# A hybrid encoder layer on one core: normalising x after the projections instead of before

## The chip, the cores and the metric

The kernel runs on one core of one Trainium2 chip. The metric is the device time of one execution in microseconds (us), lower is better. Five engines run side by side, each through its own instructions in order, and wait for one another by semaphores: PE (TensorE, matrix products; its weight loads are shown as PEld), DVE (VectorE, elementwise work), ACT (ScalarE, elementwise functions and copies), POOL (GpSimd) and SP (SyncE, which here only issues DMA transfers).

## The reference

One layer over x (1024 tokens, 1024 channels), all in float32. Cut to what matters:

```python
h = x * rsqrt(mean(x*x, axis=-1) + EPS) * norm_g           # RMS norm, one factor per token
proj = h @ w_in                                            # 1024 x 3328 columns
hy_in, g_h, q, k, v, g_a = split(proj)                     # 1536, 512, 512, 128, 128, 512
u = conv_b + sum(pad(hy_in)[:, j:j+L] * conv_w[j] for j in range(3))
hv, hx1, hx2 = split(u, 3)                                 # 512 channels each
z = hx1 * long_conv(hv, k_f[0], bias[0])                   # two-sided filters, by FFT in the reference
z = hx2 * long_conv(z, k_f[1], bias[1])                    # k_f from a three-layer sine MLP over positions
y_a = windowed_sink_attention(rope(rms(q)), rope(rms(k)), v)   # each query sees +-128 tokens
y = concat([rms(z) * silu(g_h), rms(y_a) * silu(g_a)])
out = x + y @ w_out
```

The factor rsqrt(mean(x*x)+EPS) belongs to a token, that is to a row of h, so it can be applied to x or to the rows of proj: `(x * norm_g * r) @ w = r * ((x * norm_g) @ w)`.

## The kernel before

Every float32 product of the projections is made of three matmuls: a value is split into a high part that the fast matmul format holds exactly and the low rest, and hi\*hi, hi\*lo and lo\*hi are added up in PSUM. x is loaded transposed (channels on the 128 partitions) in two halves of 512 tokens, each as 8 chunks of 128 channels. `prepare_x` squares the chunks of a half on ACT (L134, L137), adds the squares on DVE (L138), sums over channels with a matmul by ones (L142), makes the rsqrt on DVE by three Newton steps (`rsqrt`, L71 to L87), spreads it over the partitions by a matmul with the identity (`xr`, L149), and then for each chunk multiplies x by it (DVE L154), rounds to the high part `h` (ACT L158) and subtracts for the low part (L160, in turn on DVE and POOL). Only then can a projection of that half begin.

A projection tile is 128 of the 3328 columns (`half`, L192): 24 matmuls of 512 tokens for each half, into one of two PSUM banks `proj`. Its weights are loaded, split and stored in one of three slots (`weights`, L163). A hyena tile (12 of them, three for each quarter of 128 channels) is copied out of PSUM by ACT (L214), convolved with the three short taps (ACT L218, DVE L220), transposed on PE (`uT`, L230), copied by ACT (L231) and stored to DRAM as `hy`. A gate tile (8) goes through SiLU on ACT (L244, L245). Three q/k/v tiles of 256 columns are copied out by ACT (L290). Beside them the *hyena branch* works: the filter MLP (L332 to L350), and for each quarter two filter spectra (`gen` L403, `dft` L417) and two long convolutions (`fw` L532, much DVE work in the frequency domain, `inv` L571). The third stage is the attention (`smax`, `st`, `pv`) with the output projection (`po`).

The order of the program is written by `weave`: it takes pieces of the hyena branch (a) and of the projection tiles (b) in turn, by a planned cost of each piece, so that b fills PE while a waits for DVE. A scheduling layer then orders each engine's instructions by priority and its own cost model; on the chip each engine keeps that order. What precedes the weave (loading x, the MLP, the first weights, `prepare_x`) is put in order by the string `PLAN`.

## Time and profile before

| | |
|---|---|
| median of 3 runs | 689.33 us (685.95 to 689.79) |
| the profiled execution: its time, its span | 686.11 us, 684.3 us |
| mean granted TensorE clock | 0.985 |
| PE, DVE, ACT, POOL busy | 93%, 77%, 42%, 8% of the span |
| first 40 us: PE, DVE, ACT busy | 14.4, 22.8, 22.0 us |
| 200 to 300 us: PE, DVE, ACT busy | 100.0, 93.9, 35.9 us |

The span is what the trace covers; the time of the same execution is 1.8 us longer. Start times in the trace are counted from the span's start. A matmul's row lasts longer than its share of PE, since matmuls overlap: what one costs in a row of them is the distance from start to start.

### The profile page before, as it was taken

How to read it: one execution, taken by the hardware profiler on the slowest of the kernel's cores; microseconds unless marked ns; L12 is line 12 of the kernel's file. 1: busy time of each engine (PE TensorE's matmuls, PEld its weight loads, DVE VectorE, ACT ScalarE, POOL GpSimd, SP SyncE). 2: the span in 40 equal slices, each digit the busy share in tenths (PEclk: the TensorE clock that was granted, in tenths of full speed). 3: DMA queues.
4: the chain of work that ended last, by engine and by line, in shares of the span. 5: the costliest groups of instructions: out<-in, count | busy, mean ns of one | idle time of the engine just before them, and what ended most of it. 6: DMA issues, size and time to landing. Idle time of an engine off the chain costs nothing.

```text
span 684.3 us, 10610 instructions
## 1 busy us (share of the span) xinstructions
PE 634.8 (93%) x3962; PEld 559.3 (82%) x3962; DVE 525.5 (77%) x1161; ACT 287.8 (42%) x549; POOL 57.0 (8%) x65
## 2 busy tenths in 40 slices
PE   1389899999699999999999999898999899999997
PEld 1356789999589999898999998787888788888886
DVE  3878789698697999979989788353988778966431
ACT  6456343225242323433352434676587534443210
POOL 1242011012010100210100111010000000000000
PEclk9999999999899999999999999999999699999999
DMA  8943634235545314762550745654355732222321
GB/s 288 255 103 82 211 107 108 94 70 117 195 101 154 76 49 139 185 153 78 124 201 1 198 120 151 218 149 129 106 166 161 239 108 79 84 92 95 124 93 61
DMA packets 46888, 90.13 MB, mean 132 GB/s; under 512 B 7154, under 2 KB 15986, under 8 KB 46580
## 3 DMA queue, kind: packets, MB, share of 16 engines
q1 hardware_dynamic: 36656, 73.22, 31.9%
q0 software_dynamic: 7488, 13.63, 11.6%
q10 hardware_dynamic: 2692, 2.60, 1.3%
q8 instruction: 31, 0.51, 0.3%
q14 instruction: 21, 0.17, 0.1%
HBM read 53.78 MB, written 22.02 MB: 111 GB/s over the span
## 4 chain that ended last, share of the span: by engine, by line
PE 74%; DMA 15%; ACT 3%; issue 3%; DVE 3%; POOL 1%; SPq 0%; POOLq 0%; DVEq 0%; ACTq 0%
PE proj L199 8%; PE proj L198 8%; PE proj L200 8%; PE pv L758 5%; PE fw L532 5%; PE dft L417 5%; PE po L845 4%; PE po L846 4%; PE po L847 4%; DMA w_lo<-wraw 4%; PE inv L571 4%; PE qkv L285 3%; PE qkv L286 3%; PE qkv L287 3%; DMA wraw<-in_w_in 2%
## 5 line engine op out<-in xcount | busy, mean ns | idle before, releaser
L199 PE MATMUL proj<-h,w_hi 128*128 128x512 f32 x320 | 128.8, 402 | 1.8 <-DVE h L160 1.0
L198 PE MATMUL proj<-h,w_hi 128*128 128x512 f32 x320 | 127.4, 399 | 2.9 <-ACT h L158 2.9
L200 PE MATMUL proj<-h,w_lo 128*128 128x512 f32 x320 | 126.9, 396 | 0.0
L177 POOL DMA_DIRECT2D w_lo<-wraw x52 | 45.0, 865 | 398.5 <-ACT w_lo L176 343.9
L199 PEld LDWEIGHTS proj<-h,w_hi 128*128 128x128 f32 x320 | 60.7, 190 | 16.3 <-DVE h L160 2.1
L198 PEld LDWEIGHTS proj<-h,w_hi 128*128 128x128 f32 x320 | 60.6, 190 | 15.1 <-ACT h L158 4.0
L200 PEld LDWEIGHTS proj<-h,w_lo 128*128 128x128 f32 x320 | 60.8, 190 | 12.3 <-issue 1.0
L174 ACT CAST w_hi<-wraw 128x512 fp32r<-128x512 f32 x52 | 32.2, 620 | 74.5 <-DMA wraw<-in_w_in 42.4
L286 PE MATMUL qkv<-w_lo,h 128*128 128x256 f32 x192 | 54.6, 284 | 0.0
L285 PE MATMUL qkv<-w_hi,h 128*128 128x256 f32 x192 | 54.6, 284 | 0.0
L287 PE MATMUL qkv<-w_hi,h 128*128 128x256 f32 x192 | 54.4, 283 | 0.0
L758 PEld LDWEIGHTS pv<-vv,pf 128*128 128x128 f32 x352 | 48.2, 201 | 2.3 <-PE bT L720 0.2
L758 PE MATMUL pv<-vv,pf 128*128 128x66 f32 x352 | 47.9, 279 | 0.0
L417 PE MATMUL dft<-eo,d 128*128 128x128 f32 x352 | 46.6, 275 | 0.0
L417 PEld LDWEIGHTS dft<-eo,d 128*128 128x128 f32 x352 | 43.4, 192 | 0.4
L707 DVE CUSTOM_DVE_ANT_0 mj<-smax,mask 128x384 f32<-128x384 f32 (+1 forms) x64 | 33.3, 521 | 13.5 <-PE smax L702 10.4
L176 ACT ACTIVATE w_lo<-wraw 128x512 fp32r<-128x512 f32 x52 | 32.7, 628 | 10.5 <-PE qkv L286 10.5
L532 PE MATMUL fw<-u,d 128*128 128x128 f32 x256 | 33.7, 286 | 3.6 <-DMA u<-hy 3.5
L285 PEld LDWEIGHTS qkv<-w_hi,h 128*128 128x128 f32 x192 | 36.8, 191 | 0.2
L286 PEld LDWEIGHTS qkv<-w_lo,h 128*128 128x128 f32 x192 | 36.8, 192 | 0.1
L287 PEld LDWEIGHTS qkv<-w_hi,h 128*128 128x128 f32 x192 | 36.8, 191 | 0.0
L744 ACT ACTIVATE pf<-st 128x768 f32<-128x768 f32 (+1 forms) x32 | 24.2, 758 | 27.1 <-DVE st L742 24.3
(197 smaller groups left out, 1423.1 us busy)
## 6 DMA issues: line engine op xcount, KB each, us to landing
wraw<-in_w_in SPq DMA_DIRECT2D x52, 256.0 KB, 3.0
w_lo<-wraw POOLq DMA_DIRECT2D x52, 256.0 KB, 3.6
hy<-hraw SPq DMA_DIRECT2D x12, 512.0 KB, 2.6
x<-in_x_t SPq DMA_DIRECT2D x8, 512.0 KB, 5.6
dec<-in_decay SPq DMA_DIRECT2D x8, 512.0 KB, 4.4
g<-hy SPq DMA_DIRECT2D x8, 512.0 KB, 4.3
gt<-graw SPq DMA_DIRECT2D x16, 256.0 KB, 3.4
woraw<-in_w_out SPq DMA_DIRECT2D x16, 256.0 KB, 3.3
```

Of the source, the lines that this page charges most:

```text
L176: nc.scalar.mul(l, raw, -1.0)
L177: nc.gpsimd.dma_start(l.bitcast(F32), raw, accum_op=ALU.add)
L198: nc.tensor.matmul(pt, hi[:, k], xh, start=k == 0, stop=False)
L199: nc.tensor.matmul(pt, hi[:, k], xl, start=False, stop=False)
L200: nc.tensor.matmul(pt, lo[:, k], xh, start=False, stop=k == 7)
L285: nc.tensor.matmul(pt[:, b], hh, hi[:, :, k], start=k == 0, stop=False)
L286: nc.tensor.matmul(pt[:, b], hh, lo[:, :, k], start=False, stop=False)
L287: nc.tensor.matmul(pt[:, b], hl, hi[:, :, k], start=False, stop=k == 7)
L417: nc.tensor.matmul(out, m, eo[:, t, e], start=n == 0, stop=n == len(terms) - 1)
L532: nc.tensor.matmul(pt[:, k, c], self.d[:, t + k, c], u[:, t + k], start=True, stop=True)
L707: V.tensor_tensor_reduce(out=junk[:, 0:nk], in0=pm[:, 0:nk], in1=mask, op0=ALU.add, op1=ALU.max, scale=1.0, scalar=NEG, accum_out=mx[:, 4 ...
L758: nc.tensor.matmul(pv[:, h], probs[:, n, cols], self.vv[:, k0 + n, g], start=n == 0, stop=n == nk - 1)
```

## The change

x is no longer normalised before the projections. `x_high` and `x_low` split x times `norm_g` chunk by chunk as it lands (high part of even chunks on ACT, of odd ones on DVE, all low parts on DVE), and the projections run on that. The sum of squares is still made (`x_square`, in place, two chunks at a time; `x_add`; `x_sum`), and one `rsqrt` for all 1024 tokens gives `rstd` and, spread over the partitions, `row`. Each projection's result is multiplied on its way out of PSUM: hyena and gate tiles on DVE by `row` (`scaled`), where ACT copied or applied SiLU before; q/k/v tiles on ACT by `rstd`, in pieces of 256. The first hyena tiles are written out by hand in `prelude`, half by half of the tokens, with the products of the low weights last for the first two, and `in_order` pins every engine to the written order there. Three banks of the hyena branch and a third staging buffer hold the results until `row` is there. The weave starts at the fourth tile with `AHEAD` units of b counted as done. The transposes of a hyena tile are issued after the first half of the next tile (`put_off`, `late`). The constants come in one transfer, the MLP's bias and frequency are applied by ACT, the first weights are loaded between the chunks of x, and the tables `dft`, `decay`, `dft_neg` after the second half of x.

```diff
-PLAN = "cXYmWwdenabaMMbMMwvv"
...
+AHEAD = 31.2
+
+LATE = 0
...
+    def in_order(self, start):
+        last = {}
+        info = mybir.DependencyInfo(mybir.DependencyClass.NoSync, mybir.DependencyReason.DATA)
+        for i in self.nc.cur_bb.bb.instructions[start:]:
+            if i.engine in last:
+                self.tc.add_manual_dep(i, last[i.engine], info, reason="in_order")
+            last[i.engine] = i.name
...
-        self.gx = cp.tile([P, 8], F32, name="gx")
-        nc.scalar.dma_start(self.gx, a["norm_g"])
...
+        pk = cp.tile([P, 192], F32, name="consts")
+        nc.scalar.dma_start(pk, a["consts"])
...
-    def load_x(self, h, xp):
...
-    def prepare_x(self, h, xp, ps):
...
+    def load_x(self, xp, raw):
+        a, q = self.a, self.nc.sync
+        self.xt = [xp.tile([P, 8, 512], F32, tag="x", name=self.nm("x"), bufs=2) for _ in range(2)]
+        ct = [c for c, _ in self.order[:2]]
+        for h in range(2):
+            for k in range(0, 8, 2):
+                q.dma_start(self.xt[h][:, k : k + 2], a["x_t"][h][:, k : k + 2])
+                if h == 0 and k < 4:
+                    q.dma_start(raw[0][:, 2 * k : 2 * k + 4], a["w_in"][ct[0]][:, 2 * k : 2 * k + 4])
+            if h == 0:
+                q.dma_start(raw[1], a["w_in"][ct[1]])
+    def x_high(self, h, k, e):
+        out, x, g = self.h[h][:, 0, k], self.xt[h][:, k], self.gx[:, k : k + 1]
+        if e == self.nc.vector:
+            e.tensor_scalar(out=out, in0=x, scalar1=g, scalar2=None, op0=ALU.mult)
+        else:
+            e.mul(out, x, g)
+    def x_low(self, h, k):
+        self.nc.vector.scalar_tensor_tensor(
+            out=self.h[h][:, 1, k], in0=self.xt[h][:, k], scalar=self.gx[:, k : k + 1],
+            in1=self.h[h][:, 0, k].bitcast(F32), op0=ALU.mult, op1=ALU.subtract,
+        )
+    def x_square(self, h, k):
+        x = self.xt[h][:, k : k + 2]
+        self.nc.scalar.activation(x, x, AF.Square)
+    def x_add(self, h, k):
+        x = self.xt[h]
+        o, i = (x[:, 0:2], x[:, k : k + 2]) if k else (x[:, 0], x[:, 1])
+        self.nc.vector.tensor_tensor(out=o, in0=o, in1=i, op=ALU.add)
+    def x_sum(self, h, out):
+        for t in range(4):
+            self.nc.tensor.matmul(
+                out[:, 4 * h + t, 0:1], self.xt[h][:, 0, t * P : (t + 1) * P], self.ones[:, 0:1], start=True, stop=True
+            )
+    def x_rows(self, rstd, ps):
+        nc = self.nc
+        for h in range(2):
...
+            nc.scalar.copy(self.row[:, h], row)
+        nc.scalar.copy(self.rstd, rstd)
...
+    def half(self, w, h, evac, lo_last=False, bank=None):
         nc = self.nc
         hi, lo = (x[:, 0] for x in w)
-        pt = self.pj.tile([P, 512], F32, tag="proj", name=self.nm("proj"))
+        pt = (bank or self.pj).tile([P, 512], F32, tag="f" if bank else "proj", name=self.nm("proj"))
         for k in range(8):
             xh, xl = self.h[h][:, 0, k], self.h[h][:, 1, k]
             nc.tensor.matmul(pt, hi[:, k], xh, start=k == 0, stop=False)
             nc.tensor.matmul(pt, hi[:, k], xl, start=False, stop=False)
-            nc.tensor.matmul(pt, lo[:, k], xh, start=False, stop=k == 7)
-            if k < 7 and k % FINE == FINE - 1:
+            if not lo_last:
+                nc.tensor.matmul(pt, lo[:, k], xh, start=False, stop=k == 7)
+            if (k < 7 or lo_last) and k % FINE == FINE - 1:
                 yield 0.65 * FINE
+        for k in range(8 if lo_last else 0):
+            nc.tensor.matmul(pt, lo[:, k], self.h[h][:, 0, k], start=False, stop=k == 7)
+        if h == LATE:
+            self.late()
         evac(h, pt)
         yield 0.65 * min(FINE, 8)
+    def scaled(self, out, pt, h):
+        self.nc.vector.tensor_tensor(out=out, in0=pt, in1=self.row[:, h], op=ALU.mult)
+    def late(self):
+        while self.put_off:
+            self.put_off.pop(0)()
     def hyena_tile(self, n, s, sp, ps):
+        raw = sp.tile([P, S], F32, tag="raw", name=self.nm("hraw"))
+        def evac(h, pt):
+            self.scaled(raw[:, 512 * h : 512 * h + 512], pt, h)
+        yield from self.project(4 * n + s, evac)
+        self.short_conv(n, s, raw, sp, ps)
+    def prelude(self, sp, xp, raw, mlp, w0, ps, tables):
+        nc = self.nc
+        V, A = nc.vector, nc.scalar
+        self.ahead = []
+        del self.order[:2]
+        w = [self.first_slot() for _ in range(2)]
+        for k in range(0, 8, 2):
+            self.x_high(0, k, A)
+            if k < 4:
+                half = slice(2 * k, 2 * k + 4)
+                hi, lo = (x[:, 0, half] for x in w[0])
+                A.copy(hi, raw[0][:, half])
+                nc.gpsimd.tensor_tensor(out=lo, in0=raw[0][:, half], in1=hi.bitcast(F32), op=ALU.subtract)
+            if k == 6:
+                A.copy(w[1][0][:, 0], raw[1])
+            self.x_high(0, k + 1, V)
+            self.x_low(0, k)
+            self.x_low(0, k + 1)
+            if k:
+                self.x_square(0, k - 2)
+        A.mul(w[1][1][:, 0], raw[1], -1.0)
+        nc.gpsimd.dma_start(w[1][1][:, 0].bitcast(F32), raw[1], accum_op=ALU.add)
+        raws = [sp.tile([P, S], F32, tag="raw", name=self.nm("hraw")) for _ in range(3)]
+        banks = {}
+        def part(n, h, last=False):
+            def evac(h, pt):
+                banks[n, h] = pt
+            return self.half(w[n], h, evac, lo_last=last, bank=None if (n, h) in ((0, 0), (1, 0), (2, 1)) else ps)
+        def scaled(n, h):
+            self.scaled(raws[n][:, 512 * h : 512 * h + 512], banks.pop((n, h)), h)
+        def all_of(g):
+            for _ in g:
+                pass
+        all_of(part(0, 0, True))
+        b0 = part(1, 0, True)
+        for _ in range(4):
+            next(b0)
+        self.x_high(1, 0, A)
+        self.x_square(0, 6)
+        for k in range(0, 8, 2):
+            if k:
+                self.x_high(1, k, A)
+            self.x_high(1, k + 1, V)
+            self.x_low(1, k)
+            self.x_low(1, k + 1)
+        all_of(part(0, 1))
+        for k in range(0, 8, 2):
+            self.x_square(1, k)
+        next(mlp)
+        for k in (2, 4, 6, 0):
+            self.x_add(0, k)
+        next(mlp)
+        w.append(self.weights(*self.order.pop(0)))
+        tables()
+        ss = ps.tile([P, 8, 2], F32, tag="g", name=self.nm("xss"))
+        self.x_sum(0, ss)
+        all_of(b0)
+        next(mlp)
+        for k in (2, 4, 6, 0):
+            self.x_add(1, k)
+        b1 = part(1, 1)
+        next(b1), next(b1)
+        self.x_sum(1, ss)
+        next(mlp)
+        r = self.rsqrt(xp, ss[:, :, 0:1].rearrange("p a b -> p (a b)"), 8, 1.0 / DM)
+        next(mlp)
+        all_of(b1)
+        self.x_rows(r, ps)
+        next(mlp)
+        self.ahead.append(self.weights(*self.order.pop(0)))
+        for n in range(2):
+            for h in range(2):
+                scaled(n, h)
+        all_of(part(2, 0))
+        self.short_conv(0, 0, raws[0], sp, ps)
+        for _ in mlp:
+            pass
+        for _ in w0:
+            pass
+        scaled(2, 0)
+        all_of(part(2, 1))
+        scaled(2, 1)
+        self.late()
+        self.short_conv(1, 0, raws[1], sp, ps)
+        self.short_conv(2, 0, raws[2], sp, ps)
+    def short_conv(self, n, s, raw, sp, ps):
...
+        def transposes():
+            for h in range(2):
+                pt = ps.tile([P, 4, P], F32, tag="g", name=self.nm("uT"))
+                for k in range(4):
+                    t = 4 * h + k
+                    nc.tensor.transpose(pt[:, k, :], taps[:, t], self.ident)
+                nc.scalar.copy(u[:, 4 * h : 4 * h + 4, :], pt)
+            nc.sync.dma_start(self.hy[n, s], u)
+            self.stored += 1
+        self.put_off.append(transposes)
...
-                    nc.scalar.activation(raw, pt, AF.Silu)
+                    self.scaled(raw, pt, h)
+                    nc.scalar.activation(raw, raw, AF.Silu)
...
+        if half == LATE:
+            self.late()
...
-            nc.scalar.copy(raw[:, 512 * n : 512 * n + 512], pt.rearrange("p a b c -> p (a b c)"))
+            for b in range(2):
+                j = 4 * half + 2 * n + b
+                cols = slice(512 * n + 256 * b, 512 * n + 256 * b + 256)
+                nc.scalar.mul(raw[:, cols], pt[:, b].rearrange("p b c -> p (b c)"), self.rstd[:, j : j + 1])
...
-            V.tensor_scalar(
-                out=y, in0=pt, scalar1=fb[:, l : l + 1], scalar2=fb[:, 3:4], op0=ALU.add, op1=ALU.mult
-            )
+            nc.scalar.activation(y, pt, AF.Identity, bias=bf[:, l : l + 1], scale=fb[:, 3:4])
+            yield
...
-            sp = Defaults(pool(left, "stage", 1), raw=2, sc=1)
+            sp = Defaults(pool(left, "stage", 1), raw=3, sc=1)
...
-                ta = tb = 0.0
+                ta, tb = 0.0, done
...
+                    w0, w1 = (self.filter_weights(o, fw, keep, ps) for o in range(2))
+                    start = len(nc.cur_bb.bb.instructions)
+                    self.constants(cp)
+                    raw = [xp.tile([P, 8, P], F32, tag="xw", name=self.nm("xw"), bufs=2) for _ in range(2)]
+                    self.load_x(xp, raw)
+                    next(mlp)
+                    next(w0)
+                    def tables():
+                        nc.sync.dma_start(self.d, a["dft"])
+                        nc.sync.dma_start(self.dec0, a["decay"][0])
+                        nc.sync.dma_start(self.dn, a["dft_neg"])
+                    self.prelude(sp, xp, raw, mlp, w0, ps, tables)
+                    self.in_order(start)
+                    run_all(w1)
...
-            rest = weave(hyena_branch(), chain(*(tile_of(*t) for t in order[: len(order) - LASTG + 1])), SHARE, LEAD)
+            tiles = [tile_of(*t) for t in order[3 : len(order) - LASTG + 1]]
+            rest = weave(hyena_branch(), chain(*tiles), SHARE, LEAD, AHEAD)
```

The order that the built programs have on the engines shows this at three places. First PE's start. Before (`xss` is the sum of squares, `xr` the spread factor, `proj_484` the first half of tile 0, `h_89` and `h_90` the two halves of h):

```order
L142 MATMUL xss_208<-ones,xa_185 128x1 x4
L149 MATMUL xr_229<-ident,rsy_216 128x128
L142 MATMUL xss_257<-ones,xa_234 128x1 x2
...
L198 MATMUL proj_484<-h_89,w_hi 128x512
L199 MATMUL proj_484<-h_89,w_hi 128x512
L200 MATMUL proj_484<-h_89,w_lo 128x512
...
L149 MATMUL xr_278<-ident,rsy_265 128x128 x4
L332 MATMUL mlp_307<-mlp_in 128x512
```

With the change (`proj_190` and `proj_249` are the two halves of tile 0, `proj_215` the first half of tile 1; pairs and triples stand eight times each):

```order
L221 MATMUL proj_190<-h_89,w_hi 128x512
L222 MATMUL proj_190<-h_89,w_hi 128x512
...
L228 MATMUL proj_190<-h_89,w_lo 128x512 x8
L221 MATMUL proj_215<-h_89,w_hi 128x512
...
L221 MATMUL proj_249<-h_90,w_hi 128x512
L222 MATMUL proj_249<-h_90,w_hi 128x512
L224 MATMUL proj_249<-h_90,w_lo 128x512
...
L479 MATMUL mlp_280<-mlp_in 128x512
L164 MATMUL xss_307<-ones,x_141 128x1 x4
L228 MATMUL proj_215<-h_89,w_lo 128x512 x8
L481 MATMUL mlp_322<-mh_320,mlp_in 128x512
```

PE's first instructions were the sums of squares; now they are projections, and `xss` stands behind 65 matmuls. Second, DVE inside a long convolution. Before (end of the forward butterfly, the two products with the filter's spectrum, and the short taps of a hyena tile between them):

```order
L520 SCALAR_TENSOR_TENSOR X_604<-gm_616,ml_606 128x2x128 x2
L220 SCALAR_TENSOR_TENSOR hsc_690<-hraw_689,conv_w,hsc_690 128x1023
L553 TENSOR_TENSOR Y_623<-X_604,kt_429 128x2048
L220 SCALAR_TENSOR_TENSOR hsc_690<-hraw_689,conv_w,hsc_690 128x1023
L554 TENSOR_TENSOR X_604<-X_604,kt_429 128x2048
```

With the change, at the same place of a later convolution:

```order
L666 SCALAR_TENSOR_TENSOR X_901<-gm_913,ml_903 128x2x128 x2
L354 SCALAR_TENSOR_TENSOR hsc_1480<-hraw_1417,consts,hsc_1480 128x1023
L699 TENSOR_TENSOR Y_920<-X_901,kt_817 128x2048
L354 SCALAR_TENSOR_TENSOR hsc_1480<-hraw_1417,consts,hsc_1480 128x1023
L700 TENSOR_TENSOR X_901<-X_901,kt_817 128x2048
L235 TENSOR_TENSOR hraw_1484<-proj_1495,row 128x512
L702 TENSOR_TENSOR X_901<-X_901,Y_920 128x8x128
L703 TENSOR_TENSOR X_901<-X_901,Y_920 128x8x128
L235 TENSOR_TENSOR hraw_1484<-proj_1677,row 128x512
```

The evacuations of the projections (`hraw<-proj,row`), which stood on ACT, stand between the steps of the convolution. Third, PE where the transposes of the fifth hyena tile are. Before they stood ahead of the `fw` matmuls of the third convolution:

```order
L199 MATMUL proj_1577<-h_89,w_hi 128x512
L200 MATMUL proj_1577<-h_89,w_lo 128x512
L198 MATMUL proj_1577<-h_89,w_hi 128x512
...
L230 MATMUL uT_1552<-ident,hsc_1486 128x128 x4
L230 MATMUL uT_1558<-ident,hsc_1486 128x128 x3
L532 MATMUL fw_1249<-u_1244,d 128x128 x4
```

With the change they stand inside the second half of the sixth tile:

```order
L221 MATMUL proj_1677<-h_90,w_hi 128x512
L222 MATMUL proj_1677<-h_90,w_hi 128x512
L366 MATMUL uT_1520<-consts,hsc_1480 128x128 x4
L366 MATMUL uT_1526<-consts,hsc_1480 128x128 x4
L224 MATMUL proj_1677<-h_90,w_lo 128x512
```

The transposes moved about one and a half half-tiles of projection work behind the short taps that they read.

115 lines of the change are left out of this document (27 added, 88 removed).

## The prediction

> **What bounds the kernel now.** I read the page first, then the windows by stage, the waits and the timeline of the start.
>
> ```profile
> PE 634.8 (93%) x3962; PEld 559.3 (82%) x3962; DVE 525.5 (77%) x1161; ACT 287.8 (42%) x549; POOL 57.0 (8%) x65
> 0.00:85.30 85.30, 54.02 (x239) 40.41 (x240) 60.93 (x110) 43.98 (x74) 20.89 (x23) 1.00 0.66 189
> 128.00:180.00 52.00, 46.49 (x337) 43.41 (x335) 43.72 (x84) 16.84 (x40) 5.16 (x6) 0.97 0.47 127
> 180.00:224.00 44.00, 43.77 (x267) 39.46 (x267) 37.07 (x60) 13.95 (x24) 3.44 (x4) 0.96 0.40 110
> 224.00:266.00 42.00, 42.00 (x328) 40.56 (x329) 40.83 (x77) 14.21 (x34) 1.72 (x2) 1.00 0.32 101
> 266.00:308.50 42.50, 42.50 (x276) 38.46 (x275) 38.35 (x63) 15.89 (x27) 6.88 (x8) 1.00 0.58 143
> 308.50:352.70 44.20, 43.53 (x285) 39.34 (x285) 41.55 (x65) 18.31 (x41) 3.44 (x4) 1.00 0.48 142
> 352.70:397.50 44.80, 44.79 (x343) 43.03 (x344) 39.33 (x75) 14.38 (x23) 4.30 (x5) 1.00 0.40 108
> 428.00:684.30 256.30, 244.55 (x1441) 209.13 (x1439) 160.64 (x529) 122.15 (x241) 3.44 (x4) 0.97 0.40 127
> ```
>
> The columns after the window's length are PE, PEld, DVE, ACT and POOL busy. From 180 to 397.5 us, one long convolution with its filter in each window, PE has no gap to speak of; DVE is 84 to 97% busy. In the attention, from 428 us, PE is 95% busy and DVE 63%. So PE sets the pace with DVE close behind, and what PE loses at the start is lost for good. There it waits:
>
> ```profile
> PE xss L142 <- DVE xa L138: 14.0, 1, 14.0
> PE xr L149 <- DVE rsy L87: 10.1, 2, 6.2
> PE proj L198 <- ACT h L158: 2.9, 3, 1.6
> 39.35 0.63 PE L198 MATMUL proj<-h,w_hi 128*128 128x512 f32 x1
> 39.77 0.58 PE L199 MATMUL proj<-h,w_hi 128*128 128x512 f32 x1
> 40.42 0.39 PE L198 MATMUL proj<-h,w_hi 128*128 128x512 f32 x1
> 40.65 0.40 PE L199 MATMUL proj<-h,w_hi 128*128 128x512 f32 x1
> ```
>
> 24 us go by for the sum of squares and its rsqrt, and until 40 us a projection matmul costs 0.42 us from start to start, afterwards 0.23.
>
> **The start, step by step.** x arrives as before, so I take its pace from when ACT could use the last chunk of half 0 and the first of half 1:
>
> ```profile
> 5.78 0.63 ACT L134 ACTIVATE xa<-x 128x512 f32<-128x512 f32 x1 [3.08 <-DMA gx<-in_norm_g]
> 9.90 0.63 ACT L137 ACTIVATE xsq<-x 128x512 f32<-128x512 f32 x1 [0.70 <-DMA x<-in_x_t]
> 13.99 0.63 ACT L134 ACTIVATE xa<-x 128x512 f32<-128x512 f32 x1 [0.81 <-DMA x<-in_x_t]
> 19.57 1.15 ACT L137 ACTIVATE xsq<-x 128x512 f32<-128x512 f32 x2 [1.29 <-DMA x<-in_x_t]
> L154 DVE SCALAR_TENSOR_TENSOR x<-x,gx,xr 128x512 f32<-128x512 f32 x16 | 11.6, 736 | 0.0
> L346 DVE TENSOR_SCALAR my<-my 128x512 f32<-128x512 f32 x3 | 1.3, 422 | 0.1
> L556 DVE TENSOR_TENSOR X<-X,Y 128x1024 f32<-128x1024 f32 x8 | 9.8, 1222 | 0.1
> L138 DVE TENSOR_TENSOR xa<-xa,xsq 128x512 f32<-128x512 f32 x14 | 9.7, 691 | 6.4 <-ACT xsq L137 5.7
> L344 DVE SCALAR_TENSOR_TENSOR my<-mk,my 128x512 f32<-128x512 f32 x3 | 2.0, 681 | 0.0
> L84 DVE TENSOR_TENSOR rst<-rsy 128x8 f32<-128x8 f32 x6 | 1.0, 164 | 0.1
> tab<-in_rope ACTq DMA_DIRECT2D x1, 256.0 KB, 5.4
> ```
>
> The first half MB was there by 5.8 us, 2 MB by 9.9, 3 MB by 14.0, 4.5 MB by 19.6. With the change 0.5 MB of weights and the 0.3 MB of a rope table with its factors, whose issue ACT's queue now does first of all, come with half 0, so it is there at 12.5 us and half 1 at 21. DVE needs for two chunks one high part (0.42, as L346) and two low parts (0.74, as L154), 1.9 us: half 0 is split at 14.4, half 1 (four times 1.9, from 16.7, when ACT's first high part is there) at 24. PE's last 24 matmuls on half 0 (8 low-weight ones of tile 0, 16 of tile 1) take some 7 us, half of the time at the slow pace: 21.5. The 24 on half 1 end with the splitting, at 25.
>
> Then DVE leads: `x_add` three times 1.22 and once 0.69, 4.35 us for each half; the MLP's five operations 2.6 us for each layer (two as L344, three as L346); the rsqrt twelve small ones of 0.16, 2 us. In the pinned order 24 + 4.35 + 2.6 + 4.35 + 2.6 + 2 = 40. PE behind it runs the MLP's layers, `xss`, the second tile's rest, and the third MLP layer waits for ACT's sine until 38.6; then 0.95, 12 matmuls 2.7 and the eight `xr` some 1.8: 44. The tables, behind x on SP's queue, are issued about 24 us and come well before the dft. From there PE has its operands: 48 matmuls of tile 2 at 0.227 and one `e0p` (0.95) end at 56. Tile 2 ended at 96.3 before, but PE had by then done more of the hyena branch, so I compare at one point of equal work: the first `fw` and dft done, the first half of tile 3 and 8 matmuls more. That is 103.5 us before:
>
> ```profile
> 85.30 1.13 PE L532 MATMUL fw<-u,d 128*128 128x128 f32 x8 [2.59 <-DMA u<-hy]
> 103.54 0.39 PE L200 MATMUL proj<-h,w_lo 128*128 128x512 f32 x1
> 65.72 0.95 PE e0p L379 x2
> 73.85 7.03 DMA hy<-hraw
> 122.28 4.02 PE dft L417 x36
> 109.53 0.28 PE L285 MATMUL qkv<-w_hi,h 128*128 128x256 f32 x1
> 110.25 0.28 PE L285 MATMUL qkv<-w_hi,h 128*128 128x256 f32 x1
> ```
>
> With the change from 56: `e0p` 0.95, 24 + 8 projection matmuls 7.3; 44 instructions of dft, 32 of `fw`, 16 transposes and 16 of `gen` at the 0.112 of the dft row, 12.1; and some 2 us of waiting for `u`, which goes through DRAM as before (between nothing and the 7 us that its store took last time): 78.3. **PE gains 25.2 us.** The short half 0 first, the pinned order and the moved tables are in this sum; the single constants transfer and the MLP's scaling on ACT (three operations like L245 below, 0.72 each) hide in it behind DVE, uncovered 2 us.
>
> **What the change adds later.** From tile 3 on every evacuation of a hyena or gate tile costs DVE an operation:
>
> ```profile
> L405 DVE TENSOR_TENSOR eo<-gen,dec 128x512 f32<-128x512 f32 x32 | 20.9, 681 | 0.8 <-PE gen L404 0.5
> L214 ACT COPY hraw<-proj 128x512 f32<-128x512 f32 x24 | 14.0, 583 | 20.3 <-PE proj L200 15.7 <-DMA hy<-hraw 4.5
> L245 ACT ACTIVATE graw<-graw,gn 128x512 f32<-128x512 f32 x16 | 11.5, 721 | 0.2
> 113.90 0.89 PE inv L571 x8
> 422.69 1.06 PE inv L571 x8
> ```
>
> An operation out of PSUM like it is L405, 0.68 us, of ACT's copy 0.58. The Trainium skill speaks against the move ("VectorE: DVE Perf Modes", Specifications: VectorE sits closer to SBUF, ScalarE closer to PSUM), and the two rows agree: the 18 evacuations counted next would cost 10.5 us by ACT's row and cost 12 by DVE's, on an engine with less room. By the built order 18 stand between the first and the last `inv`: 18 x 0.68 = 12 us, 1.7 for each of seven convolutions. DVE had 240.9 us in the six windows from 128 to 397.5, 40.1 each; now 41.8. PE's share: first `inv` at 78.3 + 16 projection matmuls and 181 of q/k/v (0.12 each: six between the two rows above) = 103.6, against 113.9, and its last at 422.7 - 25.2 = 397.5 if it never waits: 42.0 each. DVE would be 99.6% busy. The fullest window before is 97% (40.83 of 42.0), so I take 41.8 / 0.97 = 43.1, which costs 7 x 1.1 = **7.6 us** of the gain. The bounds: nothing, if DVE fits, and 33 us, if it is no fuller than its mean before (240.9 / 269.5 = 89%, 46.8 each). The 12 q/k/v evacuations stay on ACT, each now two pieces of 256 by a factor (by L245 some 0.4 each) for one copy like L214, and hide, with ACT some 35% busy; uncovered, 12 x 0.2, 2 us.
>
> The late transposes remove one wait and move a store:
>
> ```profile
> PE uT L230 <- DVE hsc L220: 5.5, 1, 5.5
> ```
>
> It is in the 128 to 180 window, the longest. The next convolution there needed its input through SP's queue at 174 to 180 us anyway, so I credit nothing; bounds 0 and 5.5. In the attention stage 14 evacuations more on DVE (9.5 us) lie in its 37% of idle time.
>
> **Sum:** span 684.3 - 25.2 + 7.6 = 666.7, with the 1.8 us around it 668.5. The profiled execution (686.11) lies near the lowest of the runs, 3.2 us under their median, and so may this.
>
> **Rivals.**
> *PE keeps all of it.* DVE's idle before was waiting for PE (from 180 us on PE has no gap), so it may fill up freely; with the transposes' wait gone too, 686.1 - 25.2 - 0 to 5.5 = 655 to 661. Against it: 99.6%.
> *The branch falls behind.* The projections are ahead by 15 us of work, and where they have run ahead PE lacks filler: an average of 44.2 us for a convolution costs 15 us: 676. For it: a butterfly is a chain of DVE operations that nothing shortens.
> *The clock stays slow.* PE, paced by DVE chunk by chunk, is never busy long enough and keeps 0.42 us from start to start: the 24 matmuls from 14.4 end at 24.5, the next 24 at 35 instead of 25, and what hangs on them (MLP, `xr`) follows some 8 us later: 676. For it: from 27 to 40 us the rows stood at 0.63 with gaps between them; against it, the 24 in a row. The Trainium skill ("TensorE: Matmul & The Clock Gate", Part 1) says that PE starts at half clock until a window of some 3.4 us has been busy; the two distances above agree, and by that rule alone the stream from 14.4 would be released by about 21, not later.
> *Slower.* In-order DVE waits at each evacuation for its projection, with the convolution's chain behind it, and PE then waits at `inv`. The place is the second order shown. DVE stays at 89%: 668.5 - 7.6 + 33 = 694. It decides from 45.6 us for a convolution ((422.7 - 103.6) / 7, DVE 92% full). For it: ACT stood 15.7 us waiting for those same results.
> *No change that can be told*: the same at 45 us, 683 to 690.
>
> **Numbers.** The forecast (661 to 674) 0.48, all kept 0.17, branch behind or slow clock 0.18, no change 0.07, slower 0.10. A measurement of this kernel tells about 0.5%, 3.4 us, from no change: faster 0.83, same 0.07, slower 0.10. The range 655 to 684 holds the first three and leaves the two last.
>
> **What would show it.** First projection matmul near 7 us, `xr` over by 44, tile 2 by 56, the first `fw` near 70, the first `inv` near 104, then 43 us for each; DVE over 95% busy from 104 to 405 with `hraw<-proj,row` rows of 0.68; PE's first 0.23 us distance before 20 us. Wrong if the last `inv` is after 415 (DVE's waits), if half 0 is split after 17 (the transfers), or if PE has long waits on `u` or `w_lo`.

## The result, and the profile after

The changed kernel takes **708.6 us** (708.25 to 709.55) against 689.6 for the kernel before on the same chip: a ratio of 1.028, 95% interval 1.024 to 1.033. It is slower, and the forecast of 668.5 was wrong in sign. The profiled execution took 708.25 us, its span is 706.4.

The busy times of the engines on the page of the changed kernel:

```profile
PE 643.1 (91%) x3962; PEld 561.5 (79%) x3962; DVE 542.5 (77%) x1180; ACT 278.7 (39%) x525; POOL 50.2 (7%) x57
```

Three windows of it (the start to the first inverse transform, from there to the end of the last one, the rest), with the columns as before: length, PE, PEld, DVE, ACT, POOL busy, granted clock, DMA share and GB/s.

```profile
0.00:111.90 111.90, 97.58 (x552) 80.80 (x552) 86.71 (x137) 52.98 (x82) 17.47 (x19) 0.98 0.60 176
111.90:445.00 333.10, 304.11 (x1989) 275.55 (x1990) 288.75 (x506) 100.33 (x201) 29.30 (x34) 0.97 0.43 114
445.00:706.40 261.40, 241.37 (x1423) 205.12 (x1421) 167.07 (x539) 125.39 (x243) 3.47 (x4) 0.96 0.39 122
```

The same three stages of the kernel before:

```profile
0.00:113.70 113.70, 82.36 (x409) 65.59 (x410) 86.42 (x147) 56.24 (x94) 24.32 (x27) 1.00 0.61 171
113.70:428.30 314.60, 308.18 (x2118) 284.86 (x2117) 278.66 (x487) 109.40 (x214) 29.23 (x34) 0.99 0.44 121
428.30:684.30 256.00, 244.25 (x1438) 208.84 (x1437) 160.43 (x529) 122.15 (x241) 3.44 (x4) 0.97 0.40 127
```

Read the counts first. At the first inverse PE has 552 matmuls behind it where it had 409: the head start is there. At the end of the last inverse it has 2541 behind it against 2527, 16.7 us later: the head start has been used up on nothing. PE's idle time per stage is the length less the busy time: 14.3, 29.0 and 20.0 us, where it was 31.3, 6.4 and 11.8. So 17.0 us were gained at the start, and 22.6 and 8.3 lost behind it. Another 8.3 us is PE's own work: the same number of instructions is busy for 643.1 us instead of 634.8, at a lower granted clock (0.969 against 0.985).

The six longest waits of PE between the first inverse and the last, changed kernel (us in total, times, longest):

```profile
PE fw L678 <- DMA u<-hy: 9.6, 3, 6.3
PE proj L221 <- DVE hraw L235: 5.1, 3, 3.0
PE qkv L426 <- DVE hraw L235: 3.1, 2, 1.6
PE uT L366 <- DVE hsc L354: 2.8, 1, 2.8
PE dft L563 <- ACT fc L588: 2.8, 2, 2.1
PE fw L678 <- ACT fc L588: 2.7, 1, 2.7
```

and these were all of them before:

```profile
PE uT L230 <- DVE hsc L220: 5.5, 1, 5.5
PE fw L532 <- DMA u<-hy: 0.9, 2, 0.7
```

The second and third rows are of a new kind: a *projection* waits for the multiplication that empties an earlier projection's bank of PSUM. (`proj` and `qkv` take turns in two banks.) The longest of these waits, in the timelines of PE and then of DVE:

```profile
330.22 0.39 PE L222 MATMUL proj<-h,w_hi 128*128 128x512 f32 x1
330.45 0.39 PE L224 MATMUL proj<-h,w_lo 128*128 128x512 f32 x1
333.86 0.50 PE L221 MATMUL proj<-h,w_hi 128*128 128x512 f32 x1 [3.02 <-DVE hraw L235]
334.20 0.52 PE L222 MATMUL proj<-h,w_hi 128*128 128x512 f32 x1
334.51 0.63 PE L224 MATMUL proj<-h,w_lo 128*128 128x512 f32 x1
...
337.07 0.63 PE L224 MATMUL proj<-h,w_lo 128*128 128x512 f32 x1
337.50 0.50 PE L221 MATMUL proj<-h,w_hi 128*128 128x512 f32 x1
337.84 0.39 PE L222 MATMUL proj<-h,w_hi 128*128 128x512 f32 x1
```

```profile
329.16 0.69 DVE L642 TENSOR_TENSOR ml<-df 128x512 f32<-128x512 f32 x1
329.76 0.42 DVE L652 TENSOR_TENSOR X<-ef 128x256 f32<-128x256 f32 x1
...
332.44 0.76 DVE L666 SCALAR_TENSOR_TENSOR X<-gm,ml 128x256 f32<-128x256 f32 x2
333.11 0.69 DVE L235 TENSOR_TENSOR hraw<-proj,row 128x512 f32<-128x512 f32 x1
333.71 2.29 DVE L699 TENSOR_TENSOR Y<-X,kt 128x2048 f32<-128x2048 f32 x1
...
342.77 0.69 DVE L235 TENSOR_TENSOR hraw<-proj,row 128x512 f32<-128x512 f32 x1
```

One bank was complete at 325.4 us, the other at 330.8. DVE is in the middle of a butterfly, empties the first at 333.1 and the second, behind the products with the spectrum, at 342.8. PE stands still for 3.0 us; then its matmuls go up to 0.43 us from start to start until 337.8 instead of 0.23: the ten from 333.86 take 4.0 us instead of 2.3, and the granted clock from 334 to 338 us is 0.57. The Trainium skill describes such a pair ("TensorE: Matmul & The Clock Gate", section "A second HAM failure mode: psum-queue depth-cycling": PE that cycles through PSUM banks and idles briefly between groups of matmuls loses its clock again and again). At this place the trace agrees, with 3.0 us of standing and 1.7 of slow matmuls. Not every wait is followed by slow ones: after 2.7 us of waiting for `u` at 127.0 us the `fw` matmuls stand at 0.11 us from start to start, after 6.3 us at 274.8 at 0.21.

Counted in the same timelines (24 matmuls to a half tile), the last 18 hyena halves lie complete in their bank for 7.5 us on average, from the end of the last matmul until they have been taken out; before, with ACT's copies, for 1.6.

### The profile page after: what moved, and what is told of

Its sections match the earlier page's. It is cut to its first block, busy times and chain, and to the rows that moved or that the text cites. A ratio compares the mean times of both kernels' runs of the same rounds, so it can differ in the third digit from the quotient of the medians.

```text
span 706.4 us, 10583 instructions
## 1 busy us (share of the span) xinstructions
PE 643.1 (91%) x3962; PEld 561.5 (79%) x3962; DVE 542.5 (77%) x1180; ACT 278.7 (39%) x525; POOL 50.2 (7%) x57
## 4 chain that ended last, share of the span: by engine, by line
PE 49%; DVE 18%; DMA 13%; ACT 4%; issue 3%; ACTq 0%; SPq 0%; DVEq 0%
PE pv L904 5%; PE po L991 4%; PE po L993 4%; PE po L992 4%; DMA w_lo<-wraw 4%; PE proj L221 4%; PE proj L222 3%; PE proj L224 3%; PE fw L678 3%; DMA u<-hy 3%; PE qkv L426 2%; PE qkv L427 2%; PE qkv L428 2%; DMA wraw<-in_w_in 2%; PE dft L563 2%
## 5 line engine op out<-in xcount | busy, mean ns | idle before, releaser
L221 PE MATMUL proj<-h,w_hi 128*128 128x512 f32 x320 | 132.8, 415 | 12.6 <-ACT w_hi L266 7.5
L222 PE MATMUL proj<-h,w_hi 128*128 128x512 f32 x320 | 130.9, 409 | 0.8 <-DVE h L147 0.8
L224 PE MATMUL proj<-h,w_lo 128*128 128x512 f32 x304 | 122.5, 403 | 0.0
L221 PEld LDWEIGHTS proj<-h,w_hi 128*128 128x128 f32 x320 | 62.9, 197 | 27.0 <-ACT w_hi L266 7.5
L222 PEld LDWEIGHTS proj<-h,w_hi 128*128 128x128 f32 x320 | 62.5, 195 | 15.8 <-DVE h L147 4.0
L200 POOL DMA_DIRECT2D w_lo<-wraw x48 | 41.4, 862 | 411.5 <-ACT w_lo L199 392.1
L224 PEld LDWEIGHTS proj<-h,w_lo 128*128 128x128 f32 x304 | 58.4, 192 | 10.9
L197 ACT CAST w_hi<-wraw 128x512 fp32r<-128x512 f32 x48 | 29.7, 618 | 92.3 <-PE proj L222 58.9
L678 PE MATMUL fw<-u,d 128*128 128x128 f32 x256 | 36.4, 301 | 14.0 <-DMA u<-hy 11.0
L904 PEld LDWEIGHTS pv<-vv,pf 128*128 128x128 f32 x352 | 45.3, 192 | 3.5 <-PE st L883 0.9
L678 PEld LDWEIGHTS fw<-u,d 128*128 128x128 f32 x256 | 34.1, 213 | 16.4 <-issue 11.2
L904 PE MATMUL pv<-vv,pf 128*128 128x66 f32 x352 | 44.6, 271 | 0.7 <-DVE rsy L97 0.5
L890 ACT ACTIVATE pf<-st 128x768 f32<-128x768 f32 (+1 forms) x32 | 24.2, 758 | 32.1 <-DVE st L888 29.8
```

The source lines that it names most:

```text
L197: nc.scalar.copy(h, raw)
L200: nc.gpsimd.dma_start(l.bitcast(F32), raw, accum_op=ALU.add)
L221: nc.tensor.matmul(pt, hi[:, k], xh, start=k == 0, stop=False)
L222: nc.tensor.matmul(pt, hi[:, k], xl, start=False, stop=False)
L224: nc.tensor.matmul(pt, lo[:, k], xh, start=False, stop=k == 7)
L678: nc.tensor.matmul(pt[:, k, c], self.d[:, t + k, c], u[:, t + k], start=True, stop=True)
```

## The experiments

All times are medians, all ratios go against the kernel before, which took 688.9 to 689.8 us beside them.

**First: DVE's operations, or the order?** The first theory was that DVE works without a gap between a forward and an inverse transform, so that each eviction lengthens this chain by its 0.69 us. Its rivals: the put-off transposes and a blocked SP queue make `u` late (the 9.6 us above); or any new order of the filler moves the stalls about.

```diff
 # hyena_tile / gate_tiles of the change
-            self.scaled(raw[:, 512 * h : 512 * h + 512], pt, h)
+            self.nc.scalar.copy(raw[:, 512 * h : 512 * h + 512], pt)
...
-                    self.scaled(raw, pt, h)
-                    nc.scalar.activation(raw, raw, AF.Silu)
+                    nc.scalar.activation(raw, pt, AF.Silu)
```

> The change, with the hyena (from the fourth tile) and gate results evicted by ACT again: a plain copy, and SiLU straight from PSUM. The multiplication by 1/rms of these tiles is left out, so DVE has 34 operations of 0.69 us less and ACT 20 copies of 0.58 more. Chain theory (the time goes where DVE works without a gap between a forward and an inverse transform, and each eviction on DVE lengthens it): 18 x 0.69 = 12.4 us between the first and the last inverse come back, and up to 5 in the attention: 691 to 697. Order theory (put-off transposes and a blocked SP queue make u late, the evictions hide): not under 703. Luck theory (every new order of the filler moves the stalls about): anything, with stalls at other places than before and no relation to the 12.4.

**682.6 us**, ratio 0.990 (0.987 to 0.993): 26 us come back, more than the chain theory could explain with 12.4 and up to 5. (The multiplication of these tiles is left out here.)

```diff
 # short_conv of the change
-        self.put_off.append(transposes)
+        transposes()
```

> The change, with a hyena tile's transposes made at once, as in the kernel before, not half a tile later. Chain theory: the same as the change, 705 to 712. Order theory: the u transfers come earlier, the 6.3 us stall at 275 us goes and some of the 4 to 5 us lost at the early convolutions: 695 to 701. Luck theory: a move of several us either way, with stalls at other places.

**702.7 us**, ratio 1.021 (1.015 to 1.026). 6 us come back, although the first `fw` now starts at 90.1 us instead of 75.5: the transposes of the first three tiles now stand in the pinned order of the start. No theory had that.

```diff
 # hyena_tile / gate_tiles of the kernel before
-            nc.scalar.copy(raw[:, 512 * h : 512 * h + 512], pt)
+            nc.vector.tensor_tensor(out=raw[:, 512 * h : 512 * h + 512], in0=pt,
+                in1=view(self.ones, 0, [[0, 4], [1, P]]), op=ALU.mult)
...
-                    nc.scalar.activation(raw, pt, AF.Silu)
+                    nc.vector.tensor_tensor(out=raw, in0=pt, in1=view(self.ones, 0, [[0, 4], [1, P]]), op=ALU.mult)
+                    nc.scalar.activation(raw, raw, AF.Silu)
```

> The kernel before, with its hyena and gate results evicted by DVE (a multiplication by ones, same result) in place of ACT's copy and SiLU. Chain theory: 24 + 16 operations of some 0.69 us, 20 or so of them between the first forward transform and the last inverse: 700 to 709 against 689.6. Order theory: not over 694, DVE has gaps enough. Luck theory: either way, not near 689.6 + 14.

**718.0 us**, ratio 1.042 (1.037 to 1.047): 28 us more. That one edit of the change alone costs more than the whole change, and more than the chain theory's 20. The rest of the change is worth some 7 to 9 us of gain (718.0 to 708.6; 689.6 to 682.6).

Both edits of the change together (the multiplication left out again):

> The change with both: ACT evicts (multiplication by 1/rms of the later tiles left out) and the transposes made at once. What is left of the change is the early start, the shorter split and the pieces of the q/k/v evictions. Chain theory: as with ACT's evictions alone, 690 to 697. Order theory: 690 to 697 too, but then the transposes have moved it and not the evictions. If the head start of PE (25 us) were worth its time: 668 to 675. Luck theory: not the sum of the two single moves.

**692.5 us**, ratio 1.005 (1.002 to 1.008). The two single moves do not add up (-26 and -6 give 676.7): here the same step of the transposes costs 10 us. Each edit also draws a new order of the filler, and part of what it does may be that.

**Second: DVE's time, or the bank?** The chain theory now asked for 0.76 us per operation. The new one: DVE's time is not the matter, but *when* in-order DVE comes to empty the bank. To part them, ACT empties the bank and the multiplication, of the same length, is done afterwards in SBUF, on DVE as here or on POOL (`gpsimd` in the last line):

```diff
 # hyena_tile of the change, and the same for the gates ahead of their SiLU
-            self.scaled(raw[:, 512 * h : 512 * h + 512], pt, h)
+            r = raw[:, 512 * h : 512 * h + 512]
+            self.nc.scalar.copy(r, pt)
+            self.nc.vector.tensor_tensor(out=r, in0=r, in1=self.row[:, h], op=ALU.mult)
```

> The change, with every later hyena and gate result copied out of PSUM by ACT and multiplied in SBUF by DVE; the result is the reference's. DVE's work stays (34 operations of some 0.69 us), but a projection's bank is free as soon as ACT has copied it. If the loss is DVE's time as such: 704 to 712, no better than the change. If it is the bank that is kept until the in-order DVE comes to it (PE waits 8 us for evictions at the projections from 112 us to the last inverse, twice that with the clock's loss): 684 to 692.

**682.5 us**, ratio 0.988 (0.985 to 0.992). The busy times of this kernel's page:

```profile
PE 641.1 (94%) x3962; PEld 563.7 (83%) x3962; DVE 541.2 (79%) x1180; ACT 288.2 (42%) x553; POOL 46.9 (7%) x57
```

Its three stages as windows:

```profile
0.00:114.50 114.50, 98.67 (x556) 82.09 (x556) 86.62 (x137) 54.47 (x85) 14.11 (x19) 0.97 0.58 172
114.50:440.00 325.50, 316.12 (x2072) 288.29 (x2073) 291.84 (x510) 122.54 (x242) 32.74 (x38) 0.98 0.46 125
440.00:681.00 241.00, 226.26 (x1337) 193.27 (x1335) 162.70 (x535) 111.16 (x228) 0.00 (x0) 0.94 0.36 122
```

DVE's multiplication in its groups by line (busy us, mean ns of one, idle before):

```profile
L249 DVE TENSOR_TENSOR hraw<-hraw,row 128x512 f32<-128x512 f32 x18 | 12.3, 689 | 0.0
```

All waits of PE between its inverses:

```profile
PE fw L682 <- DMA u<-hy: 6.1, 2, 3.3
PE dft L567 <- ACT fc L592: 2.4, 1, 2.4
PE fw L682 <- DVE uv L596: 0.8, 1, 0.8
```

DVE is busy as long as in the change (541 and 542 us) with operations of the same 0.69 us, ACT has more to do, and 26 us are gone: exactly where nobody multiplied (682.6). So **in this kernel DVE's 34 operations cost nothing as time.** (One pair of kernels shows this; in the kernel before, further down, the same step leaves 11.6 us.) The waits for `hraw` are gone, and a half tile lies 1.0 us in its bank. 83 matmuls more are done beside the convolutions (2072 against 1989) and 86 fewer are left behind them. The stretch between the inverses is 7.6 us shorter all the same, and the one behind them 20.4 us: PE is busy there 15.1 us less (226.26 against 241.37) and idle 5.3 us less. The chain theory has fallen.

> The change, with every later hyena and gate result copied out of PSUM by ACT and multiplied by the row of 1/rms in SBUF by POOL; the result is the reference's. If the loss is DVE's 34 operations, and POOL's work does not slow DVE: 682.6 as where ACT evicted and nobody multiplied, plus 0 to 4 for the longer way to a tile's transposes: 683 to 687. If POOL's 34 operations slow DVE's beside them (1.51 us against 0.42 in one place of the kernel before): 690 to 700.

**712.0 us**, ratio 1.031 (1.028 to 1.034): worse than the change. DVE runs 1146 instructions, as many as where nobody multiplied, but is busy for 545.3 us instead of 523.2; the last section shows two of the operations that grew. How the 29 us divide between this and POOL's own length was not tried.

Only the hyena tiles' results emptied by ACT, without the multiplication, the gates by DVE as in the change:

> The change, with only the hyena tiles' results (from the fourth tile; 18 operations, all before the last inverse) copied by ACT without the multiplication; the gates' 16 stay on DVE, nearly all in the attention stage. If each DVE eviction costs the same wherever it stands (26 us for 34): 18 x 0.76 = 14 come back, 693 to 697. If only those in the convolutions' chain count: 682 to 687. If only those in the attention: 703 to 709.

**694.1 us**, ratio 1.006 (1.004 to 1.009): 14.5 us come back for the 18 hyena evictions, and by difference the other 11.5 for the gates' 16. The expectation has nearly all of these in the attention, but in this trace 8 of them start before the last inverse ends, at 444.2 us, and PE waits 3.4 us for two of these. The prediction had booked the gates at nothing.

```diff
 # short_conv: only the hand-written first three tiles keep their transposes put off
         self.put_off.append(transposes)
+        if at_once:
+            self.late()
```

> The change, with the transposes of the fourth and later hyena tiles made at once; in the first three, by hand, they stay where the change put them. Where all were made at once the first forward transform came at 90.2 us instead of 75.5 and the time fell by 6 us all the same, so here the start is kept (75 to 77) and the rest is gained: if the put-off transposes cost time in the steady part, 690 to 700; if they do not (the 6 us came from the filler's new order), 704 to 712.

**700.5 us**, ratio 1.015 (1.010 to 1.019): 8 us come back when the steady part of this kernel makes its transposes at once. The first `fw` stays at 75.6 us. Whether the transposes' place does it or the new order was not parted.

**Third: keep the bank, take the time away.** To the kernel with ACT's copies and DVE's multiplications in SBUF comes a read of one column of the bank on DVE:

```diff
             self.nc.scalar.copy(r, pt)
+            self.nc.vector.tensor_copy(self.tiny, pt[:, 0:1])
```

> The kernel in which ACT copies a result out of PSUM and DVE multiplies it in SBUF (682.5 us), and beside ACT's copy DVE reads one column of the same bank into a scratch element that nobody uses: 34 operations of 128x1, some 0.06 to 0.16 us each, 2 to 6 us in all. The result is unchanged. If the loss comes from the bank that is kept until in-order DVE comes to it, the tiny read keeps it as long as the change does: 700 to 709. If it comes from anything else (DVE's time, the way of the rows, a lucky order): 682 to 689.

**696.2 us**, ratio 1.011 (1.004 to 1.017), between the two ranges: 13.7 us of the 26 come with an operation that takes 0.15 us. Its group, two of PE's waits between the inverses, and the windows of the last two stages:

```profile
L250 DVE COPY tiny<-proj 128x1 f32<-128x1 f32 x18 | 2.7, 148 | 2.4 <-ACT hraw L249 2.4
```

```profile
PE proj L222 <- DVE tiny L250: 3.8, 3, 2.7
PE qkv L433 <- DVE tiny L250: 2.2, 2, 1.1
```

```profile
111.90:435.60 323.70, 299.91 (x1987) 270.49 (x1986) 290.06 (x530) 111.93 (x223) 29.34 (x34) 0.98 0.43 117
435.60:693.20 257.60, 243.61 (x1423) 207.21 (x1422) 166.74 (x549) 129.83 (x253) 3.48 (x4) 0.96 0.38 124
```

Its trace is the change's in three things: PE waits for the bank again, 1987 matmuls lie beside the convolutions (1989), 1423 behind them (1423). What it does not bring lies mostly in the convolutions (323.7 against 333.1 us), where the two kernels' orders differ.

The same step in the kernel before: ACT copies its hyena and gate results, and DVE multiplies them by ones in SBUF.

> The kernel before, in which ACT copies the hyena and gate results out of PSUM and DVE then multiplies them in SBUF by ones (same result). DVE has the same 40 operations more as where it evicted by itself (718 us). If the kept bank is the cause there too: 687 to 695, close to the kernel before. If DVE's time is: 712 to 720.

**700.5 us**, ratio 1.018 (1.011 to 1.024), outside both ranges: 17.5 of the 28 us come back, 11.6 stay. In that kernel ACT now waits 12.2 us for the multiplication ahead of `hsc`, and it has two staging tiles `raw` where the change has three. Between the inverses PE also waits twice for ACT at a bank, 2.4 and 2.1 us, which it never did there in the kernel before. That these make up the rest was not tried.

> The kernel in which ACT copies and DVE multiplies in SBUF (682.5 us), with the transposes of the fourth and later hyena tiles at once. With DVE's evictions this step alone brought 8 us. If it acts by itself (u is stored sooner): 672 to 678. If it only mended what the kept banks spoiled: 680 to 686. If every new order of the filler is a draw: as well 690.

**683.2 us**, ratio 0.990 (0.988 to 0.993): with ACT's copies the step that brought 8 us brings nothing.

```diff
-AHEAD = 31.2
+AHEAD = 15.0
```

> The change, with the number by which the weave counts the first three tiles as done at 15 instead of 31.2, so that projections come earlier against the hyena branch; nothing else. If the loss is the kept bank: 703 to 714, since every later eviction still waits for DVE. If the change was only an unlucky draw among the orders: under 698 or over 718.

**699.7 us**, ratio 1.016 (1.010 to 1.021). 9 us, between the two expectations; one number of the weave can do that much.

**Fourth: a third bank.** If the kept bank is what costs, one bank more should do what ACT's copies did, with every eviction left on DVE.

```diff
-NG, NF = 3, 3
+NG, NF = 2, 3
...
+    def bank(self, shape, name):
+        self.turn += 1
+        if self.turn % 3 == 2 and self.third is not None:
+            return self.third.tile(shape, F32, tag="p", name=self.nm(name))
+        return self.pj.tile(shape, F32, tag="proj", name=self.nm(name))
```

> The change with its evictions on DVE, and a third bank of PSUM for the projections until the attention begins; it is taken from the three banks that the transposes and the like share (NG 3 to 2). If the loss comes from a bank that is kept until in-order DVE comes to it, a third bank lets PE go on meanwhile: 684 to 697. If not: 702 or more, since the others have a bank less.

**682.6 us**, ratio 0.991 (0.988 to 0.994), with every eviction still on DVE. The window between its inverses, and PE's waits for a bank in it:

```profile
115.20:436.10 320.90, 309.99 (x2040) 283.39 (x2039) 290.29 (x509) 104.87 (x208) 31.10 (x36) 0.98 0.46 123
```

```profile
PE proj L221 <- DVE hraw L241: 0.7, 1, 0.7
PE qkv L432 <- DVE hraw L241: 0.4, 1, 0.4
```

A half tile still lies 9.1 us in its bank until DVE comes, but PE waits 1.1 us for it instead of 8.2, and 51 matmuls more fit beside the convolutions.

> The same third bank where ACT copies out of PSUM and DVE multiplies in SBUF (682.5 us). ACT frees a bank in time, so by the theory of the kept bank nothing is gained: 680 to 687.

**689.0 us**, ratio 1.000 (0.997 to 1.003): no gain where ACT empties the banks in time, rather 6 us lost.

> ACT copies, DVE multiplies in SBUF (682.5 us), and the weave's 31.2 is 15. With DVE's evictions this step brought 9 us. If it acts by itself (projections earlier beside the convolutions): 672 to 678. If with DVE's evictions it only drew another order: 679 to 689.

**694.7 us**, ratio 1.005 (1.001 to 1.009): 12 us *slower*, outside what was expected; the number that brought 9 us to one kernel takes 12 from the other.

The change with `NG` at 2 and nothing else:

> The change with two shared banks for transposes and the like in place of three, and no third bank for the projections: the other half of the third-bank kernel by itself. By the theory of the kept bank this alone gains nothing: 704 to 715. If it comes below 698, the third bank's result is the draw of a new order.

**709.9 us**, ratio 1.029 (1.024 to 1.033). So 27.3 us lie between two kernels that differ by the third bank alone, with the order that comes of it.

The pairs together, in us:

| otherwise like | DVE empties the bank | ACT does, DVE multiplies in SBUF | difference |
|---|---|---|---|
| the change | 708.6 | 682.5 | -26.1 |
| the change, later transposes at once | 700.5 | 683.2 | -17.3 |
| the change, 15 for 31.2 | 699.7 | 694.7 | -5.0 |
| the kernel before, with multiplications | 718.0 | 700.5 | -17.5 |
| the change, third bank | 682.6 | 689.0 | +6.4 |

In the four pairs with two banks the sign is the same. The size is not: edits that leave the evictions where they are moved the time by up to 12 us either way, and the smallest of the four differences, 5.0 us, lies within that. What remains open is how the 26 us divide between PE's waits on the chip, with the clock behind them, and the order in which PE's instructions were put at build time, which in the change and with the tiny read leaves more matmuls behind the last inverse (1423 in both, against 1337 where ACT empties the banks and DVE reads none of them). In the pair made from the kernel before, that shift is small (1449 against 1431) and the difference is still 17.5 us. The runs show both effects and do not part them.

The kernel with ACT's copy and DVE's multiplication in SBUF computes the reference's result and is faster than both: 682.5 us, 1.2% under the kernel before.

## Why the prediction was wrong, point by point

**The start: right in kind, 8 us too early.** The matmuls of half 0 begin at 7.53 us (forecast 7). Half 0 is split at 15.6 (14.4) and half 1 at 24.2 (24), though the low part takes 0.87 us where the row of another operation gave 0.74. Behind that the lateness grows: the last `xr` is out at 47.4 (44), the first `fw` comes at 75.5 (70), the first `inv` at 111.9 (103.6). The first 3.4 us of it can be read: ACT's sine is there at 40.1 instead of 38.6, and the MLP layer and the twelve matmuls between it and `xr` take 5.3 us instead of 3.65. The rest was not taken apart.

```profile
L147 DVE SCALAR_TENSOR_TENSOR h<-x,consts,h 128x512 fp32r<-128x512 f32 x16 | 13.3, 873 | 1.9 <-ACT h L144 1.9
40.12 1.48 PE L481 MATMUL mlp<-mh,mlp_in 128*128 128x512 f32 x2 [2.32 <-ACT mh L497]
41.83 0.63 PE L222 MATMUL proj<-h,w_hi 128*128 128x512 f32 x1
42.26 0.63 PE L224 MATMUL proj<-h,w_lo 128*128 128x512 f32 x1
75.52 1.13 PE L678 MATMUL fw<-u,d 128*128 128x128 f32 x8 [1.37 <-DMA u<-hy]
```

The "PE gains 25.2 us" was 17.0 by PE's idle time up to the first inverse; 8.3 us of lateness there is the same difference.

**The slow clock: rightly held unlikely where it was put, overlooked where it came.** The 0.23 us distance is there from 18.5 us, and the 24 matmuls on half 1 end at 27.6 us, not at 35 as this rival had it. But once PE had waited 2.3 us for ACT's sine, its matmuls stood at 0.43 us from start to start until 44 us (the middle rows above), with a granted clock of 0.60 from 40 to 44.3 us. This is where about half of the 3.4 us came from by which `xr` was late.

**"What PE loses at the start is lost for good": this step failed.** It took PE's 100% for the pace. Before, PE's only waits between the inverses were 6.4 us, none of them for a bank. A head start of filler is worth its time only while the filler can go on, and the change made PE wait for banks. And even where ACT frees the banks in time, little of the head start is left. In the profile of the 682.5 us kernel PE is idle 15.5 us less at the start than before, but 6.0 us more behind it, and its own work takes 6.3 us more (641.1 against 634.8) at a granted clock of 0.967 against 0.985. So the span is only 3.3 us shorter, and the medians 7.1. Why the granted clock is lower there stays open.

**The 7.6 us for the evictions: the wrong quantity.** The step charged 18 x 0.68 us to DVE's capacity, and asked whether DVE could be 97% full. (In the trace 16 evictions of hyena tiles and 6 of gates start between the first inverse and the end of the last.) As evictions the 34 operations cost 26 us; in SBUF, behind ACT's copies, they cost nothing in this kernel (682.5 against 682.6). What counted was not their length but their place in DVE's order: a bank was held 7.5 us instead of 1.6. The convolutions took (439.6 - 111.9) / 7 = 46.8 us each against 43.1, just the upper bound of 33 us, but with DVE at 288.75 / 333.1 = 87% and PE as the one that waits. The bound assumed a DVE no fuller than before, and so it came out (87% against 89%), but because PE stood waiting for banks and for `u`, not because DVE waited at the evictions: that it was met is luck. Nor do the prediction's two rows for the evictions show that DVE's operation is the longer one because it reads PSUM: with both inputs in SBUF it takes 0.689 us, with one in PSUM 0.687.

**The row that spoke and was read the wrong way.** "ACT stood 15.7 us waiting for those same results" was put down as a sign that DVE would wait too. It said that ACT was free when a result was ready, so that the bank was empty 1.6 us later on average. DVE, 87% busy, had it empty 7.5 us later. In the change DVE waited 0.2 us for those results between the first inverse and the last; they waited for DVE.

**The slower rival** had the sign and, at 694, part of the size, and gave the mechanism in reverse: DVE does not wait at an eviction for PE, PE waits at the next projection for DVE. It also stopped at the convolutions. The gates' evictions, which the prediction let lie in DVE's "37% of idle time" in the attention, were worth 11.5 us; 10 of the 16 start behind the last inverse.

**The late transposes** were credited with nothing, bounded by a gain of 5.5. With the later ones made at once, and with the order that this drew, 8 us came back in this kernel and nothing where ACT empties the banks; no bound to the other side had been given.

**The q/k/v pieces** were right: 0.47 us each, and no wait of PE on them in the steady part.

## What to carry to other kernels

When an instruction that frees a shared buffer moves to another engine, do not only price its length against that engine's idle share: ask what stands ahead of it in that engine's order, and how long the buffer then stays full against the time in which the rotation comes round. A copy by an engine that waits anyway, with the arithmetic done later, can be worth more than the operation it adds; so can one more buffer. And where the order is made by a planner, take two or three neighbouring orders of each version before believing a difference of one or two per cent.

## What the runs showed of the hardware that was not expected

POOL was no help. Its multiplication of 128x512 in SBUF took 2.7 us on average where DVE needs 0.69, and DVE's own operations grew beside it. The kernel with POOL's multiplications:

```profile
L249 POOL TENSOR_TENSOR hraw<-hraw,row 128x512 f32<-128x512 f32 x18 | 48.1, 2674 | 94.2 <-ACT hraw L248 87.9 <-issue 6.3
L356 DVE SCALAR_TENSOR_TENSOR hsc<-hraw,consts,hsc 128x1023 f32<-128x1023 f32 x24 | 35.6, 1483 | 6.8 <-ACT hsc L354 6.7
L555 DVE TENSOR_TENSOR eo<-gen,dec 128x512 f32<-128x512 f32 x32 | 20.9, 682 | 0.7 <-PE gen L554 0.7
L703 DVE TENSOR_TENSOR Y<-X,kt 128x2048 f32<-128x2048 f32 x8 | 20.4, 2546 | 0.1
```

and the change:

```profile
L354 DVE SCALAR_TENSOR_TENSOR hsc<-hraw,consts,hsc 128x1023 f32<-128x1023 f32 x24 | 30.8, 1283 | 2.4 <-ACT hsc L352 2.3
L551 DVE TENSOR_TENSOR eo<-gen,dec 128x512 f32<-128x512 f32 x32 | 21.1, 685 | 1.3 <-PE gen L550 1.1
L699 DVE TENSOR_TENSOR Y<-X,kt 128x2048 f32<-128x2048 f32 x8 | 18.3, 2290 | 0.0
```

The product with both inputs in SBUF goes from 2.29 to 2.55 us, the tap from 1.28 to 1.48, while `eo`, with one input in PSUM, stays at 0.68. The eight taps that ran beside a multiplication of a hyena tile took up to 2.33 us, the other sixteen 1.27 to 1.29. The Trainium skill describes this ("SBUF — State Buffer", section "SBUF: two separate sides": DVE and GpSimd share a pair of ports, held for a whole instruction by a GpSimd operation or, against a GpSimd operation that reads SBUF, by a DVE operation with two SBUF inputs). These rows agree with it, the untouched `eo` above all. And an operation on one column, 128x1 from PSUM, took 0.15 us; the kernel that has it in DVE's order takes 14 us longer.
